# Hybrid decoder trunk on one core: the convolution of layer 0 in 32 by 32 tiles of TensorE, without copies through memory, and a hand-written TensorE order for layer 0's first stage

## The chip, the core and the metric

One core of one Trainium2 chip runs the whole program. The metric is device time in microseconds (us) of one execution, given as the median of several. Engines: PE is TensorE (matmuls; PEld its weight loads), DVE is VectorE, ACT is ScalarE, POOL is GpSimd, SP is SyncE, which here only issues DMAs.

## The reference

Two decoder layers on 256 tokens of width 1024, all in float32. The change touches layer 0's mixer:

```python
def conv_mixer(h, w_in, b_glu, dw_w, dw_b, ln_g, ln_b, memq_g, w_out, mem_k, mem_v):
    proj = h @ w_in
    a = proj[..., :CONV_CH] + b_glu[:CONV_CH]
    gate = proj[..., CONV_CH:2 * CONV_CH] + b_glu[CONV_CH:]
    q_mem = proj[..., 2 * CONV_CH:]
    u = a * jax.nn.sigmoid(gate)
    u_pad = jnp.pad(u, ((0, 0), (CONV_WIDTH - 1, 0), (0, 0)))
    c = lax.conv_general_dilated(u_pad, dw_w[:, None, :], ..., feature_group_count=CONV_CH) + dw_b
    c = jax.nn.silu(layer_norm(c, ln_g, ln_b))
    m = memory_attention(q_mem, memq_g, mem_k, mem_v)
    return jnp.concatenate([c, m], axis=-1) @ w_out
```

CONV_CH is 768 channels, each with its own 31 taps along the tokens. The memory attention has 4 heads of 64 over 256 memory tokens, whose keys and values come from RMSNorm(mem) @ w_mem_kv. After the mixer come a residual, a dense SwiGLU of width 2816, then layer 1: a mixer with windowed attention, and top-2-of-8 expert SwiGLUs of width 3584.

## The kernel before

Channels lie on the 128 partitions, tokens along the free dimension. Large products are made of three matmuls each (`mm3`, lines 95 to 100): inputs and weights are split by `halves` (line 80) or `normed_T` (line 201) into a high part rounded by ACT and the rest from DVE, both in fp32r, and high x high, low x high and high x low are summed. Plain fp32 matmuls stand in the trace as two records each. Weights arrive in six 1 MB buffers (`raw`, SP's queue, in program order) and are split into four pairs of buffers (`split`).

Layer 0's first stage, lines 322 to 525, in the program's order: RMSNorm of the input and 16 transposes (`normed_T`); six channel tiles `c` of 128 channels in pairs, two blocks of 24 matmuls each (`pa`, `pg`), then sigmoid, product and a write of the gated tile `u` to memory (`ud`, line 395, on ACT's queue); taps and small parameters (lines 396 to 412); keys and values of the memory (`pkv`) and memory queries (`pmq`); the memory attention (`attend`, line 245, and `mem_attend`, line 292: scores `sc`, maximum, exponential, scaling, transposes `pt`, copy `pT`, values `mo`), twice two head pairs; the convolution (lines 454 to 468); the layer norm over channels (lines 472 to 510), whose sums go through TensorE (`pst`, `pcl`, `pbc`); and the output projection (`project_out`, line 308, `wo`).

The convolution of a channel tile reads `ud` back four times (line 461, ACT's queue): `sh[q]` holds, for 32 channels, four copies shifted by one token each, so that its 128 partitions are 4 taps x 32 channels. POOL builds `bands`, which hold the taps on diagonals. Then

```python
            for g in range(GT):
                for q in range(4):
                    pe.matmul(pcv[q * 32:(q + 1) * 32, :], T[:, g, q, :], sh[q][:, 4 * g:4 * g + S],
                              start=(g == 0), stop=(g == GT - 1), tile_position=(0, q * 32))
```

makes 8 groups of 4 matmuls, each with 128 rows and 32 columns of the array: four of them have the array at a time, side by side in columns.

What sets the order: the framework's planner simulates the program and orders each engine's instructions by it, so on TensorE the convolutions, the attention and the projections are mixed. A semaphore wait stops the engine that has it. `bands` has two buffers, `sh` six tiles, PSUM eight banks. The feed-forward stage (line 528 on) reads the residual after `project_out`; the experts' weights are streamed through a ring of buffers (line 724) that the two layers hold before.

Of the kernel before, what the change touches and what calls it, by code (L numbers as in the profile page):

```python
# [47 lines left out]
def hybrid_kernel(  # L48
# [118 lines left out]
    with ExitStack() as ph:  # L167
# [77 lines left out]
        def attend(qT, kT, v, nt, dst, slopes=None, sink=None):  # L245
# [3 lines left out]
            sc = [bank("sc", f"sc{par}") for par in range(2)]  # L249
            for par in range(2):  # L250
                pe.matmul(sc[par][:, :nk], qT(par), kT(par), start=True, stop=True)
            ne = nk
            nm = sm.tile([P, 2], F32, name="nm", tag="nm")
            if slopes is not None:
# [3 lines left out]
                for par in range(2):  # L258
                    dve.scalar_tensor_tensor(s[:, par, :nk], dist[:, S - nk:], -slopes[par], sc[par][:, :nk],
                                             op0=OP.mult, op1=OP.add)  # L260
                sc = [s[:, 0, :], s[:, 1, :]]
                dve.tensor_reduce(nm, s[:, :, :ne], axis=AX.X, op=OP.max, negate=True)
            else:
                for par in range(2):
                    dve.tensor_reduce(nm[:, par:par + 1], sc[par][:, :ne], axis=AX.X, op=OP.max, negate=True)
            den = sm.tile([P, 2], F32, name="den", tag="den")
            pr = wk.tile([P, 2, S + 1], F32, name="pr", tag="pr")
            for par in range(2):
                act.activation(pr[:, par, :ne], sc[par][:, :ne], AF.Exp, bias=nm[:, par:par + 1],
                               accum_out=den[:, par:par + 1])  # L270
# [10 lines left out]
            act.copy(pT[:, :nt * 2 * P], b[:, :nt * 2 * P])  # L281
            for par in range(2):
                for t in range(nt):
                    o = (t * 2 + par) * P
                    pe.matmul(dst[par * HD:(par + 1) * HD, :], v(par, t), pT[:, o:o + P],
                              start=(t == 0), stop=(t == nt - 1))

# [4 lines left out]
        def mem_attend(qT, cT, n):  # L292
            b = bank("o", "mo").rearrange("p (q n) -> p q n", n=P)
            for q in range(2):
                attend(lambda par: qT[par * HD:(par + 1) * HD, q, n * P:(n + 1) * P],
                       lambda par: mkT[par * HD:(par + 1) * HD, q, :],
                       lambda par, t: mv[:, t, (2 * q + par) * HD:(2 * q + par + 1) * HD], 2, b[:, q, :])
            evac_pair(cT[0][:, 6:8, n * P:(n + 1) * P], cT[1][:, 6:8, n * P:(n + 1) * P], b[:, 0:2, :])
# [29 lines left out]
        dram = l0.enter_context(tc.tile_pool(name="ud", bufs=1, space=bass.MemoryType.DRAM))  # L328
# [13 lines left out]
        UW = PAD + S + 6  # L342
        u = big0.tile([P, NCT, UW], F32, name="u")
        pool.memset(u[:, :, :PAD], 0.0)
        pool.memset(u[:, :, PAD + S:], 0.0)
        ud = dram.tile([NCT, P, UW], F32, name="ud")
# [8 lines left out]
        w4 = big0.tile([P, GT, 4 * NCT], F32, name="w4")  # L355
# [3 lines left out]
        win = [load_rows(cv_w_in[0][:, 0:256], KD), load_rows(cv_w_in[0][:, CH:CH + 256], KD)]  # L359

        taps = [cv[:96, 0, i * P:(i + 1) * P] for i in range(2)]
        pool.memset(taps[1], 0.0)
        small = []
        for q in range(GT):
            nj = min(4, CW - 4 * q)
            small.append((taps[q // 4][(q % 4) * 24:(q % 4 + 1) * 24, :nj * 32].rearrange("r (j n) -> r j n", n=32),
                          cv_dw_w[0][4 * q:4 * q + nj, :].rearrange("j (r n) -> r j n", n=32)))
# [5 lines left out]
        for i in range(1, 3):  # L373
            for o in (0, CH):
                for dst, src in small[:5]:
                    sp.dma_start(dst, src)
                del small[:5]
                win.append(load_rows(cv_w_in[0][:, o + i * 256:o + (i + 1) * 256], KD))
        assert not small
        memx = raw_tile().rearrange("p (t d) -> p t d", t=2)  # L380
        sp.dma_start(memx, mem[0].rearrange("(t p) d -> p t d", p=P))
        for i in range(3):
            wa, wg = [halves(m, pool if (i, j) in LOWPOOL else None, after=None)
                      for j, m in enumerate(win[2 * i:2 * i + 2])]
            for j in range(2):
                c = 2 * i + j
                pa, pg = bank("mm", "pa")[:, :S], bank("sc", "pg")[:, :S]
                for ps, w in ((pa, wa), (pg, wg)):
                    for k in range(KD):
                        mm3(ps, [m[:, k, j * P:(j + 1) * P] for m in w], [m[:, k, :] for m in x0],  # L390
                            k == 0, k == KD - 1)
                sg = wk0.tile([P, S], F32, name="sg", tag="sg")
                act.activation(sg, pg, AF.Sigmoid, bias=col("bglu", NCT + c))
                dve.scalar_tensor_tensor(u[:, c, PAD:PAD + S], pa, col("bglu", c), sg, op0=OP.add, op1=OP.mult)
                act.dma_start(ud[c], u[:, c, :])
        pw = bank("tp", "pw")
        for q in range(2):
            pe.transpose(pw[:, q * 96:(q + 1) * 96], taps[q], ident[:96, :96])
        dve.tensor_copy(w4.rearrange("p g r -> p (g r)"), pw[:, :192])
        pc = bank("tp", "pc")  # L400
# [48 lines left out]
        for n in range(2):  # L449
            mem_attend(q0T, c0, n)  # L450
# [720 lines left out]
```

## Time and profile before

| what | before |
|---|---|
| time, median of 3 runs | 1365.73 us (1364.86 to 1366.31) |
| the profiled execution's own time | 1362.78 us |
| its span, first to last instruction | 1361.1 us |
| mean granted TensorE clock | 0.980 |
| PE busy | 1286.2 us, 94% |
| DVE busy | 387.5 us, 28% |
| ACT busy | 298.7 us, 22% |
| POOL busy | 70.7 us, 5% |
| read from memory | 417.37 MB |

How to read it: all times in rows are from the span's start. A busy share over the whole span is a mean over stages with different limits, so a stage is read by itself. Matmul records overlap, since matmuls are pipelined and several can have parts of the array; the pace is read from the starts of consecutive records. PEclk is the granted clock as a share of 2.4 GHz. A wait is put down to the event that came last.

### The profile page before, as it was taken

The page shows a single profiled execution, that of the slowest core. Times are in us where ns is not written, and L with a number is a line of the kernel's source. Part 1 is how long each engine was busy: PE and PEld are TensorE (multiplying, and loading weights), DVE is VectorE, ACT ScalarE, POOL GpSimd, SP SyncE. Part 2 cuts the span into 40 slices and gives each one's busy share as a digit, 9 for nine tenths or more (in the row PEclk, how much of TensorE's full clock was granted, in tenths as well). Part 3 has the DMA queues.
Part 4 walks back from the last instruction along what each step waited for, and adds up shares of the span by engine and source line. Part 5 has one row for each costly group of instructions (what it writes and reads, how often), then busy time and mean ns, then how long its engine had stood idle before and what let it go on. Part 6 is the DMA issues. An engine that isn't in the chain of part 4 may idle for free. (4 is left out here: it accounts for less than half of the span.)

```text
span 1361.1 us, 19725 instructions
## 1 busy us (share of the span) xinstructions
PE 1286.2 (94%) x7908; PEld 720.4 (53%) x7908; DVE 387.5 (28%) x782; ACT 298.7 (22%) x575; POOL 70.7 (5%) x110
## 2 busy tenths in 40 slices
PE   6978799999898879999999999999999999999997
PEld 5844589999775643344454343444343454434443
DVE  5633465555466421012112111111110211100212
ACT  6333354444365300001111000011000111000111
POOL 4220200000031200000000000000000000000000
PEclk9989899999898988999999999999999999999999
DMA  9842145555472467989999999999999999999994
GB/s 291 291 132 72 63 149 198 184 184 184 124 223 83 191 230 299 363 336 394 413 409 409 409 412 404 409 410 412 409 409 404 411 409 408 412 411 409 403 411 199
DMA packets 137445, 420.87 MB, mean 309 GB/s; under 512 B 9658, under 2 KB 43256, under 8 KB 125048
## 3 DMA queue, kind: packets, MB, share of 16 engines
q1 hardware_dynamic: 133016, 414.39, 79.1%
q10 hardware_dynamic: 4320, 4.96, 1.1%
q8 instruction: 77, 1.26, 0.4%
q14 instruction: 32, 0.26, 0.1%
HBM read 417.37 MB, written 1.95 MB: 308 GB/s over the span
## 5 line engine op out<-in xcount | busy, mean ns | idle before, releaser
L926 PE MATMUL pa<-raw,xe 128*64 128x512 f32 x1024 | 269.8, 599 | 6.6 <-DVE hx L942 4.0
L926 PE MATMUL pb<-raw,xe 128*64 128x384 f32 x1024 | 213.2, 488 | 0.0
L982 PE MATMUL py<-raw,hT 128*64 128x512 f32 x896 | 199.3, 595 | 4.0 <-PEq L1023 1.6
L926 PEld LDWEIGHTS pb<-raw,xe 128*64 128x64 f32 x1024 | 81.1, 138 | 140.4 <-issue 140.4
L91 DVE TENSOR_TENSOR wlo<-raw,whi 128x1024 fp32r<-128x1024 f32 x108 | 131.9, 1260 | 80.8 <-ACT whi L90 80.8
L982 PEld LDWEIGHTS py<-raw,hT 128*64 128x64 f32 x896 | 67.5, 137 | 131.9 <-issue 121.4
L926 PEld LDWEIGHTS pa<-raw,xe 128*64 128x64 f32 x1024 | 77.5, 137 | 104.2 <-issue 70.0
L90 ACT CAST whi<-raw 128x1024 fp32r<-128x1024 f32 x112 | 111.5, 1046 | 54.5 <-issue 26.2
L934 PE MATMUL po<-raw,xe 128*32 128x512 f32 (+1 forms) x1024 | 116.3, 542 | 0.0
L975 DVE COPY hTo<-hto 128x224 f32<-128x224 f32 x32 | 12.5, 392 | 353.8 <-PE hto L973 353.8
L969 ACT COPY hT<-ht 128x448 f32<-128x448 f32 x32 | 17.1, 533 | 375.4 <-PE ht L967 375.4
L934 PEld LDWEIGHTS po<-raw,xe 128*32 128x32 f32 x1024 | 43.8, 109 | 55.2 <-issue 43.2
L992 PE MATMUL py<-raw,hTo 128*32 128x512 f32 x448 | 64.5, 594 | 3.3 <-PEq L1023 3.3
L942 DVE TENSOR_TENSOR hx<-s,pa 64x512 f32<-64x512 f32 x32 | 22.1, 690 | 152.6 <-ACT s L941 152.2
L958 DVE TENSOR_TENSOR hxo<-so,po 64x256 f32<-64x256 f32 x32 | 13.5, 423 | 156.8 <-ACT so L957 156.4
L941 ACT ACTIVATE s<-pa 64x512 f32<-64x512 f32 x32 | 18.9, 591 | 164.1 <-PE pa L926 163.8
L98 PE MATMUL fg<-xh,whi 128*128 128x256 f32 x176 | 50.2, 286 | 2.7 <-ACT fsg L557 2.5
L98 PE MATMUL fu<-xh,whi 128*128 128x256 f32 x176 | 50.1, 284 | 0.0
L99 PE MATMUL fu<-xh,wlo 128*128 128x256 f32 x176 | 50.1, 284 | 0.0
L100 PE MATMUL fg<-xl,whi 128*128 128x256 f32 x176 | 50.0, 284 | 0.0
L99 PE MATMUL fg<-xh,wlo 128*128 128x256 f32 x176 | 50.0, 284 | 0.0
L100 PE MATMUL fu<-xl,whi 128*128 128x256 f32 x176 | 49.9, 284 | 0.0
(297 smaller groups left out, 1620.4 us busy)
## 6 DMA issues: line engine op xcount, KB each, us to landing
raw<-in_sw_we_gate_dram SPq DMA_DIRECT2D x128, 896.0 KB
raw<-in_sw_we_up_dram SPq DMA_DIRECT2D x128, 896.0 KB
raw<-in_sw_we_down_dram SPq DMA_DIRECT2D x96, 1024.0 KB
raw<-in_sw_we_down_dram SPq DMA_DIRECT2D x32, 512.0 KB
raw<-in_cv_w_gate_dram SPq DMA_DIRECT2D x11, 1024.0 KB
raw<-in_cv_w_up_dram SPq DMA_DIRECT2D x11, 1024.0 KB
raw<-in_cv_w_down_dram SPq DMA_DIRECT2D x11, 1024.0 KB
raw<-in_cv_w_in_dram SPq DMA_DIRECT2D x7, 1024.0 KB
```

Of the source, the lines that this page charges most:

```text
L90: act.copy(hi[:, i:i + step], v[:, i:i + step])
L91: (low or dve).tensor_tensor(lo[:, i:i + step], v[:, i:i + step], hi[:, i:i + step].bitcast(F32), op=OP.subtract)
L98: pe.matmul(ps, ah, bh, start=first, stop=False)
L99: pe.matmul(ps, al, bh, start=False, stop=False)
L100: pe.matmul(ps, ah, bl, start=False, stop=last)
L926: pe.matmul(ps[half * HD:(half + 1) * HD, :c1 - c0], x, v[:, c0:c1], start=(k == 0), stop=(k == KD - 1), tile_position=(0, half * HD))
L934: pe.matmul(po[q * 32:(q + 1) * 32, :c1 - c0], x, v[:, k % 2, c0:c1], start=(k == 0), stop=(k == KD - 1), tile_position=(0, q * 32))
L941: act.activation(s[:HD, :], pa[:HD, :], AF.Silu)
L942: dve.tensor_tensor(hx[:HD, :], s[:HD, :], pa[HD:, :], op=OP.mult)
L969: act.copy(hT, b[:, :3 * P + HD])
L982: pe.matmul(py[n][n * HD:(n + 1) * HD, :], hT[:, o:o + HD], w[q // 2][:, q % 2, n * 512:(n + 1) * 512], start=(p == 0 and q == 0), stop=(p ...
L992: pe.matmul(py[n][r:r + 32, :], hTo[:, o:o + 32], w[q // 2][:, q % 2, n * 512:(n + 1) * 512], start=(i < 2), stop=(i >= NR * BLK - 2), til ...
```

## The change

It drops the copies through memory. The convolution of a channel tile is made of 32 x 32 matmuls on `u` as it lies: for each tap `j` and each group `r` of 32 channels, one matmul with rows and moving data from partitions 32 r on, and output columns 32 q with q = j mod 4. The four row groups write to four PSUM banks, the four values of q to four groups of 32 partitions, so every bank holds four partial sums. ACT and DVE copy the four banks to SBUF (`part`), and four matmuls with `eye4` (four unit matrices stacked) add the partial sums (`pf`). The scaled unit matrices `T` have one buffer. `pcv` takes four PSUM banks; attention scores and the output projection take the same four later.

The stage becomes a set of steps (generators with `yield` between parts), called in an order written by hand inside `tc.manual_schedule` for TensorE: there, TensorE keeps the program's order. The other engines are still ordered by the planner. The gated pairs load the gate before the other half; memory, its weights and the query weights are loaded ahead of the last gated pair. The output projection holds all four weight units and four accumulators at a time. Layer 1's calls of `attend` run through the same generators without an order by hand.

```diff
-        win = [load_rows(cv_w_in[0][:, 0:256], KD), load_rows(cv_w_in[0][:, CH:CH + 256], KD)]
+        win = [load_rows(cv_w_in[0][:, CH:CH + 256], KD), load_rows(cv_w_in[0][:, 0:256], KD)]
+        taps = cv[:CW].rearrange("p c n -> p (c n)")[:, :CH]
+        small = [(taps, cv_dw_w[0])]
...
+            if i == 1:
+                memx = raw_tile().rearrange("p (t d) -> p t d", t=2)
+                sp.dma_start(memx, mem[0].rearrange("(t p) d -> p t d", p=P))
+                wkv = [load_rows(w_mem_kv[j * 512:(j + 1) * 512, :], 4) for j in range(2)]
+                wq = load_rows(cv_w_in[0][:, 2 * CH:], KD)
...
-                act.dma_start(ud[c], u[:, c, :])
...
-            sh = [wk0.tile([P, UW - 4], F32, name="sh", tag="sh", bufs=6) for _ in range(4)]
-            for q in range(4):
-                act.dma_start(sh[q], bass.AP(tensor=ud.tensor, offset=ud[c, 32 * q, 0:1].offset,
-                                                  ap=[[1, 4], [UW, 32], [1, UW - 4]]))
-            pcv = bank("cv", "pcv")[:, :S]
-            for g in range(GT):
-                for q in range(4):
-                    pe.matmul(pcv[q * 32:(q + 1) * 32, :], T[:, g, q, :], sh[q][:, 4 * g:4 * g + S],
-                              start=(g == 0), stop=(g == GT - 1), tile_position=(0, q * 32))
-            act.activation(cv[:, c, :], pcv, AF.Identity, bias=col("dwb", c))
...
+        def conv(c):
+            pool.tensor_tensor(T[:, :CW], eye4[:, None, :].to_broadcast([P, CW, 32]),
+                               w4[:, c, :CW, None].to_broadcast([P, CW, 32]), op=OP.mult)
+            pcv = psx[-1].tile([P, 4, 512], F32, name="pcv", tag="cv", bufs=1)
+            for g in range(GT):
+                for r in range(4):
+                    for q in range(4):
+                        j = 4 * g + q
+                        if j < CW:
+                            pe.matmul(pcv[q * 32:(q + 1) * 32, r, :S], T[r * 32:(r + 1) * 32, j, :],
+                                      u[r * 32:(r + 1) * 32, c, j:j + S], start=(g == 0), stop=(j + 4 >= CW),
+                                      tile_position=(r * 32, q * 32))
+            part = wk0.tile([P, 4, S], F32, name="part", tag="part", bufs=1)
+            act.copy(part[:, 0:2, :], pcv[:, 0:2, :S])
+            dve.tensor_copy(part[:, 2:4, :], pcv[:, 2:4, :S])
+            yield
+            pf = bank("tp", "pf")[:, :S]
+            for r in range(4):
+                pe.matmul(pf[r * 32:(r + 1) * 32, :], eye4, part[:, r, :], start=True, stop=True,
+                          tile_position=(0, r * 32))
+            act.activation(cv[:, c, :], pf, AF.Identity, bias=col("dwb", c))
+            yield
...
+        with tc.manual_schedule(engines={mybir.EngineType.PE}):
+            run(glu(0), glu(1))
+            small_params()
+            run(glu(2))
+            cs = [conv(c) for c in range(NCT)]
+            next(cs[0])
+            wkv = [halves(m) for m in wkv]
...
+            g = glu(3)
+            next(g)
+            next(cs[0])
+            run(g)
+            next(cs[1])
+            mT = normed_T(memx, rsm, "memg", memx)
+            kn = [mem_kv(mT, wkv, 0)]
+            next(cs[1])
+            wq = halves(wq)
+            conv_mean()
+            qn = [mem_q(wq, 0)]
+            next(cs[2])
+            kn.append(mem_kv(mT, wkv, 1))
+            next(cs[2])
...
+            pairs, done0 = mem_attend(q0T, c0, 0, psc[:, 0, 256:], two)
+            a0, a1 = pairs
+            next(a0)
+            next(a1)
+            conv_sums(5)
+            rstd = conv_rstd()
+            next(a0)
+            next(a1)
+            next(a0)
+            pairs, done1 = mem_attend(q0T, c0, 1, psc[:, 1, 256:], two)
+            a2, a3 = pairs
+            next(a2)
+            next(a1)
+            done0()
+            conv_spread(*rstd)
...
+            done1()
+            w = {(n, i): unit0(n, i) for i in range(2) for n in range(2)}
...
+            for j in range(6):
+                for n in range(2):
+                    for t in range(2):
+                        wo(j, n, t)
+            ssum = new_sums()
+            for n in range(2):
+                for t in range(2):
+                    for j in range(6, 8):
+                        wo(j, n, t)
+                rsf = [add_residual(acc[n, t], t, n, ssum) for t in range(2)]
```

Between the parts shown, the order goes on in the same way: gated tile 4 with convolution 3 between its two blocks, queries of token block 1, gated tile 5 with convolution 4 between its blocks, the layer norm's sums of four tiles, convolution 5. A step `glu` is two blocks of 24 matmuls, gate first.

## Rows read from the trace of the kernel before

**Rows 1.** Windows: us, busy (count) by engine, PEclk, DMA share, GB/s

```profile
12.87:30.40 17.53, 15.96 (x107) 15.04 (x107) 10.37 (x13) 11.83 (x17) 10.41 (x4) 1.00 0.90 286
...
53.80:124.30 70.50, 57.77 (x485) 32.29 (x483) 28.37 (x48) 26.21 (x54) 13.84 (x12) 0.93 0.51 148
124.30:143.76 19.46, 14.53 (x140) 8.42 (x137) 5.18 (x16) 7.18 (x16) 0.95 (x2) 0.95 0.05 16
...
166.20:340.00 173.80, 168.71 (x1191) 158.12 (x1190) 91.00 (x113) 77.00 (x108) 0.57 (x1) 0.99 0.52 175
...
505.00:1340.00 835.00, 821.34 (x4836) 351.81 (x4830) 125.14 (x296) 85.89 (x188) 0.00 (x0) 1.00 1.00 398
```

**Rows 2.** PE's longest wait; then ACT's issues of `sh`, ns min/median/max

```profile
PE pcv L466 <- DMA sh<-ud: 11.7, 7, 3.8
...
L461 ACTq DMA_DIRECT2D sh<-ud x24: 514/516/2972, 41.1 to 124.6; - x24
```

**Rows 3.** Timeline of PE, projection: start us, us, operation [idle before]

```profile
143.76 0.80 PE L98 MATMUL wo<-whi,ch 128*128 128x512 f32 x1 [2.04 <-ACT ch L289]
...
155.24 0.40 PE L99 MATMUL wo<-whi,cl 128*128 128x512 f32 x1
...
165.72 0.39 PE L100 MATMUL wo<-wlo,ch 128*128 128x512 f32 x1
```

**Rows 4.** The convolution: a stretch of PE's timeline; all its records

```profile
57.01 3.23 PE L466 MATMUL pcv<-sh,bands 128*32 128x256 f32 x56 [1.68 <-DMA sh<-ud]
...
L466 PE MATMUL pcv<-sh,bands x384: 377/379/637, 54.6 to 133.0; 128*32 128x256 f32 x192
```

**Rows 5.** Timeline of PE: column tiles that start together

```profile
134.87 0.40 PE L483 MATMUL pst<-csq,ones 128*32 128x256 f32 x1
...
134.89 0.40 PE L483 MATMUL pst<-cv,ones 128*32 128x256 f32 x1
...
135.11 0.38 PE L483 MATMUL pst<-csq,ones 128*32 128x256 f32 x1
```

**Rows 6.** Timeline of PE: scores, two row tiles, two records each

```profile
99.19 0.70 PE L251 MATMUL sc<-mkT,mqT 64*128 64x256 f32 x4
```

**Rows 7.** Instruction groups to 175 us: busy us, mean ns | idle before

```profile
L457 POOL TENSOR_TENSOR bands<-eye,w 128x1024 f32<-128x1024 f32 x6 | 13.5, 2253 | 49.3 <-PE pcv L466 42.9 <-DVE cols L402 6.4
...
L274 DVE TENSOR_SCALAR pr<-pr,rden 128x256 f32<-128x256 f32 x8 | 4.2, 569 | 0.1
...
L269 ACT ACTIVATE pr<-sc,nm 128x256 f32<-128x256 f32 x8 | 3.8, 474 | 11.4 <-DVE nm L265 11.3
...
L265 DVE TENSOR_REDUCE nm<-sc 128x1 f32<-128x256 f32 x8 | 3.3, 417 | 7.7 <-PE sc L251 7.7
...
L281 ACT COPY pT<-pt 128x512 f32<-128x512 f32 x4 | 2.3, 586 | 1.3 <-PE pt L279 1.3
...
L269 ACT ACTIVATION_READ_ACCUMULATOR pr<-sc,nm 128x1 f32 x8 | 1.6, 195 | 0.0
...
L269 ACT ACT_TABLE_LOAD x1 | 1.3, 1283 | 1.3 <-DMA sh<-ud 1.3
```

**Rows 8.** Timeline of DVE, stage's end: residual, square sum, scaling (two)

```profile
166.15 0.69 DVE L302 TENSOR_TENSOR h<-wo,h 128x512 f32<-128x512 f32 x1 [2.27 <-PE wo L100]
166.99 0.75 DVE L161 CUSTOM_DVE_ANT_0 junk<-h,ssum 128x512 bf16<-128x512 f32 x1
...
168.43 0.88 DVE L206 TENSOR_SCALAR xn<-h,rt 128x512 f32<-128x512 f32 x2 [0.68 <-POOL rt L164]
```

**Rows 9.** Timeline of PE: starts of two blocks, 24 matmuls apart

```profile
39.23 0.28 PE L98 MATMUL pg<-xh,whi 128*128 128x256 f32 x1
...
42.11 0.28 PE L98 MATMUL pa<-xh,whi 128*128 128x256 f32 x1
```

**Rows 10.** Windows, a stretch at the lower clock

```profile
142.00:148.70 6.70, 4.94 (x12) 3.80 (x13) 4.37 (x12) 5.11 (x12) 3.98 (x6) 0.50 0.00 1
```

**Rows 11.** Timeline of DVE: the input's last low chunk

```profile
27.31 0.49 DVE L218 SCALAR_TENSOR_TENSOR xl<-xt,cols,xh 128x256 fp32r<-128x256 f32 x1 [0.54 <-ACT xh L217]
```

More of the change, by code (lines that the diff above doesn't have):

```diff
@@ L243, in hybrid_kernel, with attend @@
         big1 = None
-        def attend(qT, kT, v, nt, dst, slopes=None, sink=None):
+        def attend(qT, kT, v, nt, dst, slopes=None, sink=None, banks=None):
             nk = nt * P
-            sc = [bank("sc", f"sc{par}") for par in range(2)]
+            sc = [(banks[par] if banks else bank("sc", f"sc{par}"))[:, :nk] for par in range(2)]
             for par in range(2):
-                pe.matmul(sc[par][:, :nk], qT(par), kT(par), start=True, stop=True)
+                pe.matmul(sc[par], qT(par), kT(par), start=True, stop=True)
             ne = nk
@@ L382, in hybrid_kernel @@
[L382 to L394, printed above, removed]
-                act.dma_start(ud[c], u[:, c, :])
@@ new lines, in conv_spread @@
+        def conv_spread(mr, rv):
+            pbc = bank("mm", "pbc")
+            for i, v in enumerate((rv, mr)):
+                for t in range(2):
+                    pe.matmul(pbc[:, i * S + t * P:i * S + (t + 1) * P], v[:, t:t + 1].to_broadcast([P, P]), ident,
+                              start=True, stop=True)
+            for c in range(NCT):
+                y = cv[:, c, :]
+                dve.tensor_tensor(y, y, pbc[:, :S], op=OP.mult)
+                dve.tensor_tensor(y, y, pbc[:, S:], op=OP.subtract)
+                act.activation(y, y, AF.Silu, scale=col("lng", c), bias=col("lnb", c))
+                evac_pair(c0[0][:, c, :], c0[1][:, c, :], y, pool)
@@ L434, in hybrid_kernel, with mem_q @@
                        [(0, 4, kn.rearrange("p (n d) -> p n d", d=HD))])
-            heads_T(kn, 2, "hmk", mkT, t)
-        c0 = pair_tile("c")
-        wq = halves(load_rows(cv_w_in[0][:, 2 * CH:], KD))
-        q0T = big0.tile([P, 2, S], F32, name="mqT")
-        for t in range(2):
+            return kn
+        def mem_q(wq, t):
             ps = bank("mm", "pmq")
@@ L485, in hybrid_kernel @@
-        st = wk0.tile([P, S], F32, name="st", tag="sg")
-        act.copy(st, pst)
-        pcl = bank("o", "pcl")
-        for t in range(2):
-            pe.matmul(pcl[:, 2 * t:2 * t + 2], st[:, t * P:(t + 1) * P], pick, start=True, stop=True)
-        pcl = pcl[:, 0:4].rearrange("p (t q) -> p q t", q=2)
-        mr = sm.tile([P, 2], F32, name="mr", tag="mr")
-        dve.tensor_scalar_mul(mr, pcl[:, 0, :], 1.0 / CH)
-        m2 = sm.tile([P, 2], F32, name="m2", tag="m2")
-        dve.tensor_tensor(m2, mr, mr, op=OP.mult)
@@ L619, in hybrid_kernel @@
                 for n in range(2):
-                    mem_attend(mq1T, c1, n)
+                    pairs, done = mem_attend(mq1T, c1, n, bank("o", "mo"))
+                    for pair in pairs:
+                        for _ in pair:
+                            pass
+                    done()
         slope = [2.0 ** (-8.0 * (i + 1.0) / QH) for i in range(QH)]
```

238 lines of the change are left out of this document (142 added, 96 removed).

## The prediction

> **What bounds the kernel now.** I read the stretches of the span by stage first [rows 1]. Three things are to be seen there. The feed-forward stage (166 to 340 us) is TensorE's: 168.7 of 173.8 us busy, DMA at 0.52. The expert stage (505 to 1340 us) is DMA's: share 1.00 at 398 GB/s. The first stage, up to 166.1 us, is neither's: from 53.8 to 124.3 us TensorE is idle for 12.7 us and DMA has a share of 0.51, and from 124.3 to 143.8 us it is idle for another 4.9 us. Next I read who TensorE waited for between 53.8 and 144 us, and the tile of the shifted copies: 11.7 us of that idle time end with a copy `sh` landing from memory, and the 24 issues of these copies stand on ACT's queue, 514 ns at the median and up to 2.97 us [rows 2]. So this stage is bound by a chain of writes, reads and small statistics with TensorE waiting in between. What ends it is the output projection's last matmul, 165.72 + 0.39 = 166.1 us [rows 3].
>
> Nothing later has slack that would take up a gain: the feed-forward stage starts when its input is there and runs on TensorE, and the expert stage's stream goes into buffers that layers 0 and 1 hold until they are done. So I count what the end of the output projection moves, one to one.
>
> **The change, part by part.**
>
> *Removed.* Six writes `u` to memory, 24 reads of `sh`, their issues on ACT's queue, and the 11.7 us of waits [rows 2]. Seven of eight loads of the taps leave SP's queue; what they hid is SP's own time, I cost them at nothing. Two small POOL memsets go too.
>
> *The convolution itself.* Before, a channel tile is 8 groups of 4 matmuls, two passes each (384 records for 6 x 32 matmuls): 64 records, four at a time. The trace shows 56 of them in 3.23 us [rows 4]: 14 rounds, (3.23 - 0.38) / 13 = 0.219 us a round. Now it is 31 taps x 4 row groups = 124 matmuls, 248 records, in 16 tiles of the array. If 16 run at once, it is again 16 rounds: 15 x 0.219 + 0.38 = 3.7 us, no gain and no loss. If only four run at once, as the rows of before show it, it is 62 rounds, 61 x 0.219 + 0.38 = 13.7 us. The ends are far apart. For the low end: four column tiles start within 0.02 us of each other, with their second passes 0.24 us later [rows 5], so 16 starts would take some 0.1 us of a 0.22 us round; and two row tiles run together as well, since the four records of a score pair take 0.70 us, where one after the other would need 3 x 0.219 + 0.38 = 1.04 us [rows 6]. I take 3.7 us, and keep 13.7 us as the upper end.
>
> A page speaks against it. The Trainium skill, page "TensorE: Matmul & The Clock Gate", section "Wait — 56ns, not 53.3ns?", says that starts of matmuls never come closer than about 25 ns. By that rule (an estimate) a channel tile takes 248 x 0.025 = 6.2 us, 2.5 us more each, and the gain below shrinks by 15 us to about 1 us. This trace's starts at 0.01 us do not agree with it, for column tiles.
>
> *Added per channel tile.* A fold of four column matmuls, two passes: 0.24 + 0.38 = 0.62 us by [rows 5], 0.65 with its switch, six times 3.9 us. The four banks are copied out by ACT (0.59 us for 128x512 [rows 7]) and DVE (0.69 us [rows 8]) side by side; five of the six stand beside matmuls placed between convolution and fold for that; if that cover is gone, each costs 0.7 us. POOL's bands stay at 2.25 us each [rows 7], and now have one buffer, so they start after the previous convolution; at least 2.9 us of other matmuls lie between any two convolutions, which hides them but for the semaphores.
>
> *The new order of TensorE, summed from 12.87 us:*
> - First two channel tiles: kept as before, to 30.4 us [rows 1], 17.5 us.
> - Four more gated tiles: 24 matmuls take 42.11 - 39.23 = 2.88 us [rows 9], eight such blocks 23.0 us.
> - Six convolutions, 22.2 us; six folds, 3.9 us.
> - Memory's 16 transposes in four banks, each emptied by two ACT and two DVE operations near 0.47 us [rows 7]: an estimate of 3.5 us, a third of it idle. Small transposes: 2.2 us, an estimate from 0.70 us for four records [rows 6].
> - Keys and values: 48 matmuls of 512 columns at (165.72 - 155.24) / 46 = 0.228 us [rows 3], 10.9 us. Memory queries: 48 of 256 columns at 0.12, 5.8 us.
> - Mean and sums ahead of the attention: 1.4 + 2.8 = 4.2 us, an estimate from the pace of [rows 5].
>
> That is 93.2 us, so the last fold ends at 106.1 us. Then a chain in which TensorE mostly waits. First head pair: scores 0.70, two maxima 0.83, table load 1.28, two exponentials with their sums 1.34, two scalings 1.14, transposes about 0.70, copy 0.59, values about 0.70 [rows 6, 7]: 7.3 us. Each of three more pairs adds the longer of its ACT and DVE shares with semaphores, about 2.5 us: 7.5 us. The eight records that spread the statistics (about 1.2 us by [rows 6]) and the last evacuation (0.8 us, as two of the operations of [rows 7]) make 16.8 us. The statistics themselves now stand beside this; before, the projection's main part waited for them until 143.76 us [rows 3]. Then 96 matmuls of the projection, 21.9 us, and the half clock: before, after a stretch of waits, TensorE was granted 0.50, its lower level of 1.2 GHz, from 142.0 to 148.7 us [rows 10], and I expect such a stretch here too. In it a projection matmul takes twice its 0.228 us, so the 5 us of it that fall on the projection cost about 2.6 us. Sum: 106.1 + 16.8 + 21.9 + 2.6 = 147.4 us.
>
> *What is late next.* Token block 0 finished 24 matmuls ahead of block 1 before; now it finishes 6 matmuls (1.4 us) ahead. So DVE's residual, square sum and scaling of both blocks run back to back (each 0.69 + 0.75 + 0.88 us [rows 8]): 1.2 us more from the last matmul to the next stage. And about 1 us for copies and band builds that are not quite covered.
>
> End, counted like the old one: 149.6 against 166.1 us, **16.5 us gained**. The profiled execution took 1362.78 us (span 1361.1), so it would take 1346.3. The median of the three runs, 1365.73, lies 2.95 us above that execution; the same difference from it gives **1349.2 us**.
>
> *Other moved steps.* Loads of the memory input, its two weight halves and the query weights go ahead of the last two gated loads on SP; four projection weights need all four split buffers, the last two of which come free when the last gated tile is done, near 98 us. At 0.90 DMA share and 286 GB/s [rows 1] the 11 MB up to the last gated load are in by some 40 us, 30 us ahead of use. No cost, unless an ACT cast waits in ACT's queue for a buffer with an evacuation behind it.
>
> **Rivals.**
> 1. *The tiles don't run 16 at once (slower).* Place: the six convolutions. They decide from 16.5 / 6 = 2.75 us more each, that is from 6.4 us a channel tile, 26 ns a record. With four at once it is 10.0 us more each: 1349.2 + 60 = 1409 us. For: 16 tiles stand nowhere in this trace, and four row tiles writing four banks at once don't either. Against: [rows 5, 6]. Chance 0.12.
> 2. *Half of it.* Eight at once, or starts that come only half as fast as the array could take them: 31 rounds, 30 x 0.219 + 0.38 = 6.95 us each, 3.25 us more: 1349.2 + 19.5 = 1369 us. For: [rows 4] show no run of records closer than the array takes them. Against: the bunched starts of [rows 5]. Chance 0.12. The rule of the Trainium skill named above would end near here, at 1364 us (an estimate).
> 3. *TensorE's fixed order waits where the planner's order went round.* The last chunk of the input's low half came at 27.31 + 0.49 us, and the planner filled with other blocks [rows 11]. If it comes as late again, the first gate block ends at 28.0 us and three more blocks at 28.0 + 8.6 = 36.6 us instead of 30.4; with two more table loads in the attention the loss is 6.2 + 2.6 = 8.8 us: 1358 us. For: matmuls behind a wait now wait too. Against: the transposes now come first, so DVE can take that chunk earlier. Chance 0.14.
> 4. *The gain is hidden anyway*, the expert stream setting the time: 1365.7 us. Against: its share is 1.00 only from 505 us on, and 0.52 in the feed-forward stage [rows 1]. Chance 0.05.
>
> **How the numbers follow.** The forecast has 0.57; its own range is 1339 (attention pairs better overlapped, no half clock) to 1357 us (5 us a convolution). A measurement of this kernel can tell about 0.2%, 2.7 us, from no change. Faster: forecast and rival 3, 0.71. Same: rival 4 and half of rival 2, 0.11. Slower: rival 1 and the other half, 0.18. The range reaches to rival 2's nearer half and leaves out rival 1: 1339 to 1368 us.
>
> **What would show it.** Right: about 248 records of `pcv` in 3.7 us; no `sh` or `ud`; the last `wo` matmul near 149 us; later stages of the same length. Wrong: `pcv` records over 26 ns apart, which kills the gain; TensorE idle before the first gated tiles' blocks or for over 17 us between the last fold and the projection; or a later stage that grew by what the first one lost.

## The result, and the profile after

The changed kernel takes **1397.15 us** (median of 4 runs, 1393.1 to 1399.31) against 1365.3 us for the kernel before on the same chip: ratio 1.023, 95% interval 1.0204 to 1.0256. It is slower; 1349.2 us was forecast. The profiled execution took 1398.08 us (span 1396.4).

The windows of the changed kernel, columns as in [rows 1]:

```profile
12.87:30.40 17.53, 7.17 (x25) 5.69 (x25) 6.90 (x10) 9.32 (x16) 10.67 (x6) 0.78 0.75 260
53.80:124.30 70.50, 61.87 (x1278) 48.88 (x1278) 25.85 (x38) 24.97 (x43) 12.65 (x12) 0.98 0.28 91
124.30:171.77 47.47, 31.48 (x448) 19.66 (x447) 16.47 (x45) 23.39 (x50) 7.23 (x9) 0.72 0.14 47
200.00:385.00 185.00, 181.02 (x1260) 170.51 (x1261) 93.98 (x118) 79.81 (x112) 1.29 (x2) 0.96 0.51 177
540.00:1375.00 835.00, 821.65 (x4840) 354.41 (x4838) 125.11 (x296) 85.89 (x188) 0.00 (x0) 1.00 1.00 398
```

The expert window looks as before. The feed-forward stage is 3.1 us longer (first to last start of `fg`: 203.4 to 385.4 against 170.0 to 348.9), at a lower mean clock (0.96 against 0.99 in its window). In the first 17.5 us TensorE is busy for 7.17 us where it was 15.96; it is also idle in the third window, while the second is well filled. The end of the stage, on PE's timeline, answers to [rows 3]:

```profile
171.77 0.79 PE L98 MATMUL pwo<-whi,ch 128*128 128x512 f32 x1 [0.94 <-DVE cl L293]
...
197.25 0.39 PE L100 MATMUL pwo<-wlo,ch 128*128 128x512 f32 x1
...
203.42 0.58 PE L98 MATMUL fg<-xh,whi 128*128 128x256 f32 x1
```

The first feed-forward matmul comes at 203.4 us; before it came at 170.0. I call this the **stage end** from here on: it holds 33.4 of the 35.3 us between the two profiled executions (1398.08 and 1362.78 us). Against the forecast the stage lost time in three places.

*The start.* The queue of SP, then ACT, then DVE:

```profile
10.40 0.56 SPq L375 DMA_DIRECT2D rows<-in_cv_memq_norm_g_dram  x1
13.16 0.28 SPq L375 DMA_DIRECT2D rows<-in_cv_ffn_norm_g_dram  x1
15.90 0.27 SPq L375 DMA_DIRECT2D rows<-in_sw_attn_norm_g_dram  x1
...
16.85 0.41 SPq L77 DMA_DIRECT2D raw<-in_cv_w_in_dram  x1
```

```profile
22.06 1.99 ACT L90 CAST whi<-raw 128x1024 fp32r<-128x1024 f32 x2 [6.16 <-DMA raw<-in_cv_w_in_dram]
23.95 0.47 ACT L217 ACTIVATE xh<-xt,cols 128x256 fp32r<-128x256 f32 x1
```

```profile
32.10 0.47 DVE L218 SCALAR_TENSOR_TENSOR xl<-xt,cols,xh 128x256 fp32r<-128x256 f32 x1
```

The third weight load stands behind ten small ones and is issued at 16.85 us, where it was 9.44. ACT waits 6.16 us for it, with a chunk of the input queued behind the cast. The last low chunk is ready at 32.57 us; in [rows 11] it was 27.80. The first two gated tiles end at 43.28 us (30.4 before).

*The convolution.* One tile without a stop, and one with, on PE's timeline:

```profile
66.23 5.21 PE L441 MATMUL pcv<-u,bands 32*32 32x256 f32 x248
```

```profile
119.43 4.00 PE L441 MATMUL pcv<-u,bands 32*32 32x256 f32 x191
125.07 2.31 PE L441 MATMUL pcv<-u,bands 32*32 32x256 f32 x57 [1.64 <-issue]
```

From first start to last end the six take 9.19, 5.21, 5.53, 6.96, 7.95 and 5.56, together 40.4 us. 5.7 us of that is idle time ended by "issue".

*The chain behind the last fold*, which ends at 142.35 us. ACT, then PE:

```profile
157.71 1.28 ACT L499 ACT_TABLE_LOAD   x1
...
162.55 1.28 ACT L269 ACT_TABLE_LOAD   x1
...
164.89 1.28 ACT L499 ACT_TABLE_LOAD   x1
```

```profile
166.12 1.09 PE L280 MATMUL pt<-ident,pr 128*128 128x128 f32 x4 [5.63 <-DVE pr L274]
```

The spreading of the statistics, with its silu, comes ahead of the last head pair, so ACT changes tables back and forth and TensorE waits 5.63 us for the last pair's exponentials (`pr`). The projection starts 29.4 us after the last fold.

### The profile page after: what moved, and what is told of

Read it like the earlier page. It is cut to its first block, busy times and chain, and to the rows that moved or that the text cites. A ratio compares the mean times of both kernels' runs of the same rounds, so it can differ in the third digit from the quotient of the medians.

```text
span 1396.4 us, 21985 instructions
## 1 busy us (share of the span) xinstructions
PE 1303.8 (93%) x9064; PEld 745.4 (53%) x9064; DVE 384.4 (28%) x788; ACT 304.8 (22%) x583; POOL 68.1 (5%) x108
## 5 line engine op out<-in xcount | busy, mean ns | idle before, releaser
L91 DVE TENSOR_TENSOR wlo<-raw,whi 128x1024 fp32r<-128x1024 f32 x108 | 128.4, 1231 | 91.8 <-ACT whi L90 91.8
L1054 ACT ACTIVATE s<-pa 64x512 f32<-64x512 f32 x32 | 18.9, 591 | 164.6 <-PE pa L1039 164.3
```

The lines of the kernel that those rows point to most:

```text
L91: (low or dve).tensor_tensor(lo[:, i:i + step], v[:, i:i + step], hi[:, i:i + step].bitcast(F32), op=OP.subtract)
L1054: act.activation(s[:HD, :], pa[:HD, :], AF.Silu)
```

## The experiments

Sixteen kernels ran. Those of one group shared a chip and its runs of the kernel before (1363.06, 1365.23, 1364.87 and 1364.52 us). The stage end is read from each profile; after it, times are not comparable everywhere (see the last section). e6 and e17 leave parts of the convolution's sums out, and with other values the experts get other tokens (768 `po` matmuls where there were 1024): from the first to the last start of the experts' `pa` matmuls it is 840.2 us in e17 and 840.4 in e6, 846.5 in the kernel before. Their times are some 6 us short for that alone, so for them the stage end counts.

| run | edit | time us | ratio, 95% interval | stage end us |
|---|---|---|---|---|
| before | | 1365.3 | | 170.0 |
| the change | | 1397.15 | 1.023 [1.0204, 1.0256] | 203.4 |
| e1 | five small loads first | 1395.88 | 1.0241 [1.0222, 1.0259] | 201.5 |
| e2 | planner orders the start | 1398.45 | 1.0256 [1.0235, 1.0277] | 197.9 |
| e3 | planner orders everything | 1391.5 | 1.0204 [1.0183, 1.0225] | 195.4 |
| e4 | spreading last | 1388.2 | 1.0186 [1.0166, 1.0206] | 196.4 |
| e5 | four accumulators, planner | 1397.78 | 1.0252 [1.0221, 1.0283] | 196.5 |
| e6 | half the columns | 1386.08 | 1.0153 [1.0133, 1.0172] | 195.1 |
| e7 | old convolution, new order | 1411.89 | 1.0337 [1.032, 1.0355] | 213.4 |
| e8 | e7, e5 and e4 | 1401.36 | 1.0249 [1.0217, 1.0281] | 200.7 |
| e9 | convolutions in halves | 1398.1 | 1.0233 [1.0213, 1.0253] | 199.2 |
| e10 | other order of loads | 1395.78 | 1.0222 [1.0201, 1.0242] | 193.1 |
| e11 | e10, four accumulators | 1393.1 | 1.0191 [1.0167, 1.0215] | 193.1 |
| e12 | the new convolution alone | 1390.65 | 1.0185 [1.0164, 1.0206] | 188.7 |
| e14 | tile loops swapped | 1401.09 | 1.0274 [1.0249, 1.0299] | 204.3 |
| e15 | before, GpSimd issues `sh` | 1351.16 | 0.9904 [0.9883, 0.9925] | 156.6 |
| e16 | e11 and e4 | 1385.1 | 1.0149 [1.0126, 1.0173] | 184.3 |
| e17 | before, no copies | 1345.64 | 0.9869 [0.9848, 0.989] | 150.1 |

**What the copies were worth, and a cheaper way to get it.** e17 takes the copies out of the kernel before and leaves its records alone; e15 only moves their issue:

```diff
-                    pe.matmul(pcv[q * 32:(q + 1) * 32, :], T[:, g, q, :], sh[q][:, 4 * g:4 * g + S],
+                    pe.matmul(pcv[q * 32:(q + 1) * 32, :], T[:, g, q, :], u[:, c, 4 * g:4 * g + S],
```

> The kernel before without the copies through memory: the same 64 records a channel tile read the gated rows where they lie, so the shifts by one to three tokens are left out of the sums, as are all waits for shifted rows and 11 MB of traffic in that stretch. This is the ceiling of what taking the copies away can give. Theory (the waits removed were worth 11.7 us and little else): the first feed-forward matmul comes 8 to 12 us earlier than 170.0, at 158 to 162. Rival (another wait takes their place, the copies were hidden): less than 4 us earlier.

```diff
-                act.dma_start(sh[q], bass.AP(tensor=ud.tensor, offset=ud[c, 32 * q, 0:1].offset,
+                pool.dma_start(sh[q], bass.AP(tensor=ud.tensor, offset=ud[c, 32 * q, 0:1].offset,
```

> The kernel before with one edit: the 24 loads of shifted rows are issued by GpSimd instead of ACT. If their 11.7 us of waits came from standing in ACT's queue, they shrink to 5 us or less and the time falls by 4 to 8 us to about 1358; if they came from the six buffers and from the memory round trip, the waits stay and the time is within 3 us of 1364.

The ceiling is 19.9 us of stage, almost twice the 11.7 us of waits named for it. Another 7.1 us are TensorE's own: the same records keep it busy for 27.70 us in e17 and for 34.75 in the kernel before (shown below); their smaller pieces and the lower clock there (0.93 against 0.96) were not told apart. e15 gets 13.4 us of time with one word changed, where 4 to 8 were expected, and is faster than both kernels. Its convolution's idle time, and the issues, in the tile view (ns min/median/max, first and last start):

```profile
L466 PE MATMUL pcv<-sh,bands x384: 378/379/404, 54.8 to 119.9; 128*32 128x256 f32 x192
its engine sat idle before it (us, times) until:
  DMA sh<-ud: 2.6, 3
```

```profile
L461 POOL DMA_DIRECT2D sh<-ud x24: 677/677/1120, 41.2 to 111.2; - x24
```

An issue is dearer on GpSimd (677 ns at the median against 516 in [rows 2]), yet the waits fall from 11.7 to 2.6 us: standing in ACT's queue had made most of them. The memory round trip, which e15 keeps, was not the cause.

**What the new records cost.** e12 puts the new convolution alone into the kernel before:

```diff
-            pcv = bank("cv", "pcv")[:, :S]
+            pcv = [bank(tag, f"pcv{r}") for r, tag in enumerate(("cv", "o", "sc", "sc"))]
...
+            for r in range(2):
+                act.copy(part[:, r, :], pcv[r][:, :S])
+                dve.tensor_copy(part[:, 2 + r, :], pcv[2 + r][:, :S])
```

> The kernel before with only the convolution replaced by the 32 by 32 tiles (four existing accumulator banks, fold with the eye matrix), in the planner's order, with the old start and the old attention. Theory (the new records cost 5 us a channel tile plus 0.65 for the fold plus refills, where the old ones cost 3.3, and the waits for the shifted rows that they remove were worth about as much): within 8 us of the kernel before, 1356 to 1372. Rival 1 (the fixed order, the start and the attention's order made all of the loss): 1350 or less. Rival 2 (the new convolution itself is the loss): 1375 or more.

Rival 2 of it holds: the convolution alone loses 18.7 us of stage, 38.6 us against e17. TensorE's busy time on `pcv` in the window 40 to 155 us (second number, with the records) in e17 and in the kernel before:

```profile
40.00:155.00 115.00, 27.70 (x384) 12.56 (x384) 2.82 (x6) 0.96 0.32 107
```

```profile
40.00:155.00 115.00, 34.75 (x384) 13.62 (x384) 2.85 (x6) 0.93 0.43 130
```

The same for `pcv`, then for the fold `pf`, in e12 and in the changed kernel:

```profile
40.00:155.00 115.00, 48.17 (x1488) 25.98 (x1488) 4.56 (x12) 3.87 (x12) 0.97 0.27 92
...
40.00:155.00 115.00, 12.68 (x48) 2.91 (x48) 2.84 (x6) 0.97 0.27 92
```

```profile
40.00:155.00 115.00, 34.66 (x1488) 22.95 (x1488) 4.15 (x6) 3.52 (x6) 0.93 0.31 100
...
40.00:155.00 115.00, 4.45 (x48) 1.07 (x48) 2.84 (x6) 0.93 0.31 100
```

In e12 the convolution keeps TensorE busy for 48.17 + 12.68 = 60.85 us, or 58.7 with the overlap of the two counted once; the old records need 27.70. That is 31.0 of the 38.6 us. In the hand order it is 34.66 + 4.45 and 5.7 idle, 44.8 us. In e12 the planner mixes in small pieces, as PE's timeline shows:

```profile
119.74 1.06 PE L456 MATMUL pcv<-u,bands 32*32 32x256 f32 x16
120.73 0.62 PE L465 MATMUL pf<-part,eye 128*32 128x256 f32 x2
121.28 0.62 PE L456 MATMUL pcv<-u,bands 32*32 32x256 f32 x4
121.83 0.62 PE L465 MATMUL pf<-part,eye 128*32 128x256 f32 x2
```

Two records of the fold take 0.62 us, nearly as long as all eight in one piece (0.64 us in the changed kernel): every piece takes that time again. The hand order avoids this, but so does the planner in e3, which orders the changed kernel itself (`pcv`, then `pf`):

```profile
40.00:155.00 115.00, 37.05 (x1488) 22.36 (x1488) 4.15 (x6) 3.52 (x6) 0.95 0.30 98
...
40.00:155.00 115.00, 5.06 (x48) 1.21 (x48) 2.84 (x6) 0.95 0.30 98
```

With 2.1 us idle that is 44.2 us, no more than in the hand order. Why the pieces are small in e12 and not in e3 was not tried; the two differ in buffers and in the program's order.

Two edits ask what the rate of the records depends on:

```diff
-                            pe.matmul(pcv[q * 32:(q + 1) * 32, r, :S], T[r * 32:(r + 1) * 32, j, :],
-                                      u[r * 32:(r + 1) * 32, c, j:j + S], start=(g == 0), stop=(j + 4 >= CW),
+                            pe.matmul(pcv[q * 32:(q + 1) * 32, r, :P], T[r * 32:(r + 1) * 32, j, :],
+                                      u[r * 32:(r + 1) * 32, c, j:j + P], start=(g == 0), stop=(j + 4 >= CW),
```

> Each convolution matmul moves 128 columns instead of 256; half of the tokens are left out of the sums (the first half's results stand in both halves), everything else stays. Theory (the tile grid is bound by the rate at which loads and matmuls are delivered, near 17 to 20 ns a record plus refills of the instruction store): the six convolutions keep their 40.6 us within 4 us and the time stays within 3 us of 1397. Rival (the array or the accumulator banks bound them, each record costing its columns): they fall to about 22 us and the time to about 1380.

```diff
-                for r in range(4):
-                    for q in range(4):
+                for q in range(4):
+                    for r in range(4):
```

> In the changed kernel the two inner loops of the convolution are swapped: consecutive records go to the four row groups instead of to four column groups of one row group. Theory (each group of 16 tiles costs its columns plus the starts of its own records, whatever their order): unstalled tiles stay at 4.8 to 5.0 us for 248 records, time within 3 us of 1397. Rival (weight loads into one row group block each other): unstalled tiles fall to 3.3 to 4.0 us, time 5 to 8 us less.

A tile without a stop on PE's timeline, with half the columns (e6), and with the loops swapped (e14):

```profile
65.95 3.50 PE L441 MATMUL pcv<-u,bands 32*32 32x128 f32 x248
```

```profile
66.20 5.21 PE L441 MATMUL pcv<-u,bands 32*32 32x256 f32 x248
```

Neither theory on e6 was right as put: its six convolutions take 30.9 us, between 22 and 40. (5.21 - 0.37) / 247 = 19.6 ns a record at 256 columns, (3.50 - 0.27) / 247 = 13.1 ns at 128. If the cost is a line in the columns, 128 columns cost 6.5 ns, 256 cost 13.0, and 6.6 ns a record are left that do not depend on them. Columns alone would then be 247 x 13.0 ns + 0.37 = 3.6 us, which is the old tile: e7 has 64 old records in 3.66 us in one piece. That speaks for the line; a third length was not run. The new grid adds its fixed part, the fold and the stops.

The 6.6 ns are a mean, not something that each record shows. Of the 247 distances between starts in the tile at 66.23 us, 173 lie between 12 and 19 ns, and ten pauses of 40 to 200 ns make 1.57 us; most of these come every 0.65 us and last 0.16 us. With 128 columns 141 distances lie between 12 and 19 ns, and nine pauses make 0.52 us, most of them 0.04 us every 0.44 us. Whether the fixed part goes with each record or with each stretch of some 33 records (about two for each of the sixteen array tiles) was not tried, and its cause stays open.

The order of the tiles does not matter: e14 has the same 5.21 us and a like stage end, as its theory said, though the theory's 4.8 to 5.0 us and its 3 us of time were both missed (the time is 4 us above the change's).

e9 cuts each convolution in two with other matmuls between:

```diff
                                       tile_position=(r * 32, q * 32))
+                if g == 3:
+                    yield
```

> Every convolution is cut in two halves of about 128 records with other matmuls of the same order between them; nothing else changes. Theory (runs of about 180 or more load-and-matmul records outrun the refill of TensorE's instructions, which made gaps of 1.4 to 2.7 us): the gaps ended by issue inside the convolutions vanish, the six take about 30 us instead of 40.6, the last fold ends 6 to 9 us earlier. Rival (the refill's rate, not the length of a run, is what binds, or the gaps are caused by what else the DMA engines move): the gaps stay, the last fold ends within 3 us of 142.35.

The idle time ended by issue falls from 5.7 to 2.6 us, the last fold ends 4.1 us earlier (138.26), between theory and rival. That long runs are a cause is not shown by it: with whole runs it is 2.5 us in e10, 1.9 in e11, 2.1 in e3 and 6.5 in e4, and in e9 one stop of 1.73 us comes 20 records into a half. In the changed kernel's trace 16 KB packets of instructions move near the stops (starting at 53.9 and 57.5 us around the first), which suggests refills; but such packets also move within tiles that do not stop (at 71.0, 87.2 and 90.7 us), and refills were not tried by themselves.

**The old convolution in the new order.**

```diff
+            sh = [wk0.tile([P, UW - 4], F32, name="sh", tag="sh", bufs=6) for _ in range(4)]
+            for q in range(4):
+                act.dma_start(sh[q], bass.AP(tensor=ud.tensor, offset=ud[c, 32 * q, 0:1].offset,
+                                             ap=[[1, 4], [UW, 32], [1, UW - 4]]))
```

> The convolution alone is undone: 64 records a channel tile in column tiles with shifted copies through memory, inside the new fixed order. Theory (the 32 by 32 tiles cost 40.6 us where the old records cost about 23): if the copies come back in time behind the order's other work, the stage shortens by 10 to 18 us, time 1379 to 1387. Rival (the copies are late in the fixed order, each convolution waits 3 to 5 us for its shifted rows): time 1395 to 1410.

> The new order with the old convolution, the four-accumulator start, and the spreading moved behind the last attention pair. If the three losses are separate they add: about 11 (start) + 14 (convolution) + 8 (spreading) off 1397, that is about 1364, no slower than the kernel before. Rival: the copies through memory stand in the fixed order again, time 1375 to 1385.

Both rivals are right on the cause and too low on the time. In e7 the waits for `sh` grow to 25.9 us in 12 places, 4.3 us a convolution, and in e8 they are 20.7 us in 11 places; nothing goes around them. e7 takes 1411.89 us where its rival had 1395 to 1410, e8 1401.36 where it had 1375 to 1385. ACT issues the copies in both; whether this fixed order could live with copies that GpSimd issues, as in e15, was not tried.

**The order's own losses.** The start first:

```diff
-                for dst, src in small[:10]:
+                for dst, src in small[:5]:
```

> One edit to the changed kernel: five small parameter loads, not ten, stand ahead of each of the later weight loads on SP's queue, as before the change. Theory A (SP's queue): the third weight load is issued near 9.5 us, not 16.85 us; ACT's cast that waits for it, and the input's chunks behind that cast, come some 7 us earlier, the first two channel tiles end near 34 us, not 43.3 us, and the time falls by 7 to 11 us, to about 1388 us. Rival (TensorE's fixed order by itself holds the start): the load comes earlier but the first two tiles still end after 40 us, and the time falls by less than 3 us.

```diff
+        run(glu(0), glu(1))
         with tc.manual_schedule(engines={mybir.EngineType.PE}):
-            run(glu(0), glu(1))
```

> One edit to the changed kernel: the first two gated channel tiles stand outside the hand-written order, so the planner mixes their blocks; the small loads stay as they are in the change. Theory A (SP's queue): the third weight load is still issued at 16.85 us and the input's chunks still wait behind ACT's cast, so the tiles end at 38 us or later and the time falls by at most 5 us. Rival (the fixed order is the cause): TensorE works around the late chunks as it did before, the two tiles end near 32 us, and the time falls by about 11 us, to 1386 us.

```diff
+        p4 = psx[-1].tile([P, 4, 512], F32, name="p4", tag="cv", bufs=1)
+        run(*[glu(c, [p4[:, 2 * c + i, :S] for i in range(2)]) for c in range(2)])
```

> The first two gated tiles get four accumulators again (a four-bank tile that the convolution uses only later), the planner orders them chunk by chunk, and only five small loads stand ahead of the third weight load. Theory (the start was lost because only two accumulators were open while the input's chunks arrived, and because of the ten small loads, both together): first two tiles end near 31 us instead of 43.28, the time falls by 9 to 12 us to about 1386. Rival (the fixed order behind them or the casts of the weights, which ACT now does in another order, hold the start): they still end after 40 us and the time stays above 1393.

None was enough. In e1 the third weight load is issued at 7.72 us, but the first two tiles end only at 40.39 us, as its rival said; in e2 they end near 41.7, as its theory said; in e5 the last chunk still lands at 31.67 us behind the memory's squares on DVE, and the third tile goes ahead of the second. So the chunks themselves were late, and the order of loads came next:

```diff
             for o in (CH, 0):
-                for dst, src in small[:10]:
-                    sp.dma_start(dst, src)
-                del small[:10]
                 win.append(load_rows(cv_w_in[0][:, o + i * 256:o + (i + 1) * 256], KD))
+            if i == 1:
+                for dst, src in small:
+                    sp.dma_start(dst, src)
...
+        memx = raw_tile().rearrange("p (t d) -> p t d", t=2)
```

> Only the order of the loads on SP changes: the four input weights of the first four gated tiles go ahead of all small loads, and the memory, its weights and the query weight behind the last input weights. Theory (ACT's casts wait in order for late weights, the input's chunks stand behind them, and the memory's sums of squares delay the last chunk on DVE): the last chunk lands by 28 us instead of 32.1, the first two gated tiles end near 37 to 38 us instead of 43.28, stage 5 us shorter. Rival (the two accumulators alone set it): the first two tiles end after 41.

```diff
+            for ks, qs in ((range(4), (0,)), (range(4), (1,))) + tuple(((k,), (0, 1)) for k in range(4, KD)):
+                for k in ks:
+                    for q in qs:
+                        for c in range(2):
+                            mm3(p4[:, 2 * c + q, :S], ...)
```

> The same order of loads, and the first two gated tiles filled chunk by chunk into four accumulators by hand. Theory (late chunks and two accumulators together made the loss at the start): the first two tiles end at 30 to 32 us as in the kernel before, the first feed-forward matmul comes 10 to 13 us earlier than 203.42, time near 1386. Rival (another wait of the fixed order takes the time back): tiles early, but the stage less than 5 us shorter.

In e10 the last chunk lands at 27.22 us and the first two tiles end at 37.01, as expected; the stage ends 10.3 us earlier, more than expected. In e11 they end at 30.43 us, where the forecast had them, yet the stage ends no earlier than in e10, as its rival said: the first convolution waits. ACT, DVE, then PE:

```profile
35.61 0.63 ACT L156 ACTIVATE junk<-raw 128x512 bf16<-128x512 f32 x1 [8.66 <-DMA raw<-in_mem_dram]
...
41.18 0.48 DVE L551 SCALAR_TENSOR_TENSOR u<-p,cols,sg 128x256 f32<-128x256 f32 x1
...
41.81 7.13 PE L441 MATMUL pcv<-u,bands 32*32 32x256 f32 x248 [4.76 <-DVE u L551]
```

The memory input now arrives late, ACT waits 8.66 us for it, and the sigmoids of the first two tiles stand behind it in ACT's order. The convolution reads the first tile's row, but it waits until the second tile's product is made as well: its four PSUM banks are the ones that the four accumulators hold till then.

The attention chain, and the whole order:

```diff
-            conv_spread(*rstd)
...
             done1()
+            conv_spread(*rstd)
```

> One edit to the changed kernel: the spreading of the layer norm's statistics, and with it the six sigmoid-linear activations, stands after the last head pair in the program. Theory B (table loads and ACT's work stand inside the attention's chain): ACT loads a table three times in the chain before the change of this edit; one load of the exponentials' and one of the later activations' table remain, the last pair's exponentials no longer wait behind two activations, and the stretch from the last fold to the output projection shrinks from 29.4 to some 23 us; the time falls by 4 to 7 us. Rival (the chain of the pairs itself sets it): under 2 us, or slower, since the projection then waits for the activations.

```diff
-        with tc.manual_schedule(engines={mybir.EngineType.PE}):
+        with ExitStack():
```

> One edit to the changed kernel: no hand-written order at all; the planner orders TensorE, everything else (32 by 32 convolution, buffers, order of the program) stays. If the order is what costs most (start and attention, 12.9 and 12.6 us over the forecast), the time falls by 15 to 25 us, to 1372 to 1382 us, and the convolutions still take 5 us each or more. If the convolution's slow records cost most (18.4 us over the forecast), the time stays over 1390 us. Below 1365 us would mean that the tiles of 32 by 32 by themselves pay.

> The changed kernel with both repairs of its order: the new order of loads with four accumulators at the start, and the spreading behind the last attention pair. If the two losses are separate they add: the first feed-forward matmul at 186 to 188 us (203.42 less 10.3 and 7.0), about where the kernel with the new convolution alone has it (188.7), time 1380 to 1387. Rival (they share one cause further on): above 191 us.

e4 takes 7.0 us off the stage; the projection starts 23.4 us after the last fold instead of 29.4. In e3 the planner wins 8.0 us back; at 1391.5 us it is on the side of the convolution's slow records (over 1390), if barely. The two repairs of e16 add, with some to spare: 184.3 us against the 186 to 188 expected.

**The ledger of the stage end:** 170.0 before; 150.1 without copies (-19.9); 188.7 with the new convolution in the planner's order (+38.6); 184.3 in the fixed order with a good start and the spreading last (-4.4); 203.4 as the change has it (+19.1, of which e10 and e11 show 10.3 and e4 7.0).

## Why the prediction was wrong, step by step

- *What bounds the stage* was right: the waits for `sh` did cost what the forecast hoped to gain. The ceiling is 19.9 us by e17, and 16.5 were forecast. (The median issue of `sh` in [rows 2] is 516 ns; the 514 ns that the forecast names are the shortest.)
- *"If 16 run at once ... 3.7 us"* is the step that turned the sign. The tiles do overlap (records of some 0.4 us start 19.6 ns apart at the mean), but not at the pace of their columns alone: on top of the 13.0 ns that the columns explain, 6.6 ns a record are left at the mean, so a tile takes 5.2 us unstopped. With the stops and the slower stretches around them, which no term of the sum had, it is 6.7 on average: 40.4 us for six where 22.2 were summed, 18.2 us too little. [Rows 5] showed starts 0.02 us apart for four records; that this holds for 248 in a row did not follow. Rival 2, with 6.95 us a tile and 1369 us, came near this term partly by luck: unstopped tiles are 1.7 us faster than it said, and the rest are stops that it did not name. The fold was nearly right (4.45 against 3.9 us); its two copies, forecast side by side, run one after the other (0.59 us on ACT, then 0.69 on DVE).
- The rule of the Trainium skill, page "TensorE: Matmul & The Clock Gate", section "Wait — 56ns, not 53.3ns?", was set aside. It gave 6.2 us a tile (an estimate); measured are 5.2 unstopped and 6.7 with stops. As a floor of 25 ns between starts the trace does not bear it out (19.6 ns); as a warning it was nearer than my sum.
- *"First two channel tiles: kept as before, to 30.4 us"* failed by 12.9 us. I costed the moved loads on SP at nothing but ACT's casts; nearly that exception came (the cast waited for a late load, not for a buffer), and rival 3, which named the place, had only 6.2 us for it. The ten small loads ahead of the third weight were in the diff and not counted, and are 2.9 us by e1; the whole order of the loads is 6.3 us by e10, and four accumulators filled chunk by chunk in place of two give back the other 6.6 in e11. e11 ends these tiles at 30.43, so the place is right, but there 4.76 us come back as a wait of the first convolution.
- *"make 16.8 us"*, the attention chain, measured 29.4. Rival 3 had the two table loads; not counted was that the silu work itself stands ahead of the last pair's exponentials, and that TensorE, waiting so much, ran at a granted 0.61 between 142.4 and 171.77 us. With the spreading last it is 23.4; no run takes the other 6.6 us apart.
- Together: last fold 142.35 against 106.1 (36.2 us, of which start 12.9, convolutions 18.2 and smaller terms 5.1), chain 12.6, and the rest 1.1: 49.9 us from the forecast stage end (170.0 - 16.5 = 153.5), the gap of the medians being 47.95.
- *Later stages of the same length* held within 2 us for this kernel, in sum. Rival 4 was not seen: e15 carries its stage's 13.4 us through to the time. That e17's time falls by 18.9 us is in part luck: it has the second loss told below, and a shorter expert stage makes up for it.

## What to carry to other kernels

Before an operation is rebuilt to be rid of its transfers, see how much of the wait is only the queue that issues them: moving 24 issues off a busy engine's queue gave 13.4 us here, two thirds of the ceiling. A matmul cut into sixteen small tiles does the same column work with four times the records, and here it had a fixed part beside the columns (6.6 ns a record at the mean), and a finely mixed fold took 12.68 us where whole pieces took 4.45; multiply both out. A fixed order of the kind tried here keeps every late operand's wait, so its loads have to be ordered with it.

## What the runs showed that was not expected

*A second loss, 260 us later.* e2, e5, e7 to e12, e16 and e17 run a stretch in layer 1's attention at the lower clock that the kernel before and the changed kernel run at full clock. The same work in e11 and in the kernel before, some 260 us behind their stage ends (columns as in [rows 1]):

```profile
456.00:470.00 14.00, 14.00 (x45) 7.49 (x45) 7.82 (x29) 5.26 (x21) 0.94 (x5) 0.51 0.00 1
```

```profile
430.00:444.00 14.00, 13.23 (x80) 7.99 (x78) 11.77 (x43) 9.30 (x36) 1.32 (x7) 1.00 0.01 2
```

At the granted 0.51, close to the lower level of 1.2 GHz, 45 records are done where 80 were. From stage end to first expert matmul it is 326.5 us in e11 and 318.7 in the kernel before; it is 325.7 to 328.1 in the runs named, and 317.8 to 323.1 in the others. So e5 and e10 show 6.9 and 10.3 us at the stage end but hardly any in their times, and stage ends tell more than totals of this size. Both kernels wait on ACT's exponentials just ahead of it; what decides for or against the fall was not settled.

*A cost beside the columns.* At 32 by 32 a tile of 248 records takes 5.21 us where its columns explain 3.6, whatever the order of the tiles: 6.6 ns a record at the mean, by two lengths. Within a tile TensorE also stops at times, for 1.4 to 2.7 us in the changed kernel, with nothing to wait for but its issue. The cause of either stays open.
